# gMLP stage of a two-layer trunk: the split of v's normalised tiles written behind u's first block pair

## The chip, the cores and the metric

The kernel runs on one core of a Trainium2 chip. The metric is the device time of one execution in microseconds (us); for the kernel before it is the median of three runs. The profile is of one further execution.

## The reference, cut to what matters

The trunk is two layers over 512 tokens of width 1024. Layer 0 has a stick-breaking attention mixer, layer 1 a token-mixing MLP (gMLP); a SwiGLU network follows each mixer, and each of these four parts stands between two RMS norms with shift, scale and gate from a conditioning vector. The change is in layer 1's mixer:

```
def token_mixing_mixer(h, w_in, ln_g, w_s, b_s, w_out):
    B, S, D = h.shape
    uv = jax.nn.gelu(h @ w_in)
    u, v = jnp.split(uv, 2, axis=-1)
    v = layer_norm(v, ln_g)
    n = S // TM_CHUNK
    v = v.reshape(B, n, TM_CHUNK, TM_GROUPS, TM_GROUP_DIM)
    ...
    sv = jnp.einsum('gts,bnsgc->bntgc', ws, v) + b_s.T[None, None, :, :, None]
    y = u * sv.reshape(B, S, D)
    return y @ w_out
```

## The kernel before, in words

All matrix products keep float32 accuracy by splitting. A float32 tile is split into a high part (a copy into a reduced float32 type, on ScalarE) and a low part (the tile less its high part, on VectorE); a product is then three matmuls, high by high, low by high and high by low (`mm3`, line 122). Every matmul is recorded by `mm` at line 111, every ScalarE activation or copy at line 89, and nearly every VectorE operation at line 73, so that in the profile the names of the tiles tell them apart.

The gMLP stage is `gmlp`, line 1655. It runs in this order:

- v, in four tiles `vt` of 128 tokens by 1024 channels. The first 512 channels come from plain products, the last 512 by a scheme of seven block products (lines 1690 to 1707) that accumulate in three PSUM banks (`r`); each value passes through gelu.
- the statistics of the layer norm, per token (lines 1718 to 1725, `bns`, `mv`, `sd`, `r`), and the normalisation of the four `vt` tiles in place on VectorE (line 1735).
- the split of each normalised tile: high part `vnh` on ScalarE (line 1740), low part `vnl` on VectorE (`vn_low`, line 1728). The low parts of tiles 0 and 1 stand in the text right there; those of tiles 2 and 3 stand behind the first and the second block pair of u (line 1795), with an order dependency on the last VectorE operation written before them.
- u, in eight column blocks m. Block 0 was made earlier. Blocks 1 and 2, and then 3 and 4, are made as two block pairs by `u_pair` (line 1584), each with seven block products in three PSUM banks (R1, R2, R3, all named `r` in the profile). ScalarE copies three partial sums out of the banks into `e` (s1, s5, u1 of lines 1610, 1615 and 1617), VectorE combines them with what the banks hold next (lines 1612, 1619, 1621), and the bank is then accumulated on or written again by the next product. So some products can only start when such a copy or combination has read the bank. Blocks 5 to 7 are plain products (`u_unit`, line 1565).
- the mixing: `mix` (line 1746) multiplies each group of `vnh` and `vnl` with the mixing matrix `ws` into PSUM (`sv`); the first call comes behind u's block 5 (line 1800). The gating `u * sv` and the output projection (`part`, `out_proj`) follow.

Each engine executes its own instructions in a fixed order. In this stage that order is not written by hand: it is set, when the program is built, by a scheduler that starts from the text's order and each instruction's dependencies. The order of TensorE, VectorE and ScalarE is written by hand only in other stages (chains switched on at lines 1395 and 1190). Tiles called `slot` come from one pool of 28 buffers (line 45) that are handed out in the order of the text, so moving a `slot` call also shifts which buffer a tile gets.

Weights arrive by DMA on SyncE's queue (`load`, line 127), and their splits (`wh`, `wl`) are made ahead of their use on the same ScalarE and VectorE that work on v and u. Partial sums of the next layer's modulation rows (`bg.step`, tiles `acch`, `accl`, `adaps`, `A`, `B`) are mixed in.

Of the kernel before, what the change touches and what calls it, by code (L numbers as in the profile page):

```python
# [9 lines left out]
F32R = mybir.dt.float32r  # L10
AF = mybir.ActivationFunctionType
# [4 lines left out]
NT = T // P  # L16
# [19 lines left out]
def trunk(ctx: ExitStack, tc: tile.TileContext, A: dict, out: bass.AP):  # L36
# [17 lines left out]
    def nm(s):  # L54
        uid[0] += 1
        return f"{s}_{uid[0]}"

    def slot(dt, name, a=2, b=512):
        return s4.tile([P, a, b], dt, tag="s4", name=nm(name))

    def bank(name, tag="b"):
        return psum.tile([P, 512], F32, tag=tag, bufs=6 if tag == "b" else 2, name=nm(name))
# [32 lines left out]
    act = Scalar()  # L95
# [7 lines left out]
    def order(b, before):  # L103
        tc.add_manual_dep(
            b.ins, before.ins.name,
            mybir.DependencyInfo(mybir.DependencyClass.NoSync, mybir.DependencyReason.DATA),
            reason="order",
        )
# [13 lines left out]
    def mm3(o, lh, ll, rh, rl, start, stop):  # L122
        mm(o, lh, rh, start, False)
        mm(o, lh, rl, False, False)
        mm(o, ll, rh, False, stop)
# [221 lines left out]
    def wget(src, look=3):  # L347

        n = taken[0]
        taken[0] += 1  # L350
        while len(got) < min(n + 1 + look, len(stream)):
            wemit()
        assert stream[n][3] == src, (stream[n][3], src)
        return got[n]
# [199 lines left out]
    def hB(hT, k, lo, n):  # L554

        h, l = hT[lo // 256, k // 4]
        lo %= 256
        return h[:, k % 4, lo : lo + n], l[:, k % 4, lo : lo + n]
# [428 lines left out]
    with tc.tile_pool(name="att", bufs=1) as att, tc.tile_pool(name="att2", bufs=2) as att2:  # L987
# [62 lines left out]
        for js in (B31, B2, B0):  # L1050
            at, n = {}, 0
# [147 lines left out]
        for k in range(KD):  # L1199
# [9 lines left out]
            if k > 3:  # L1209
                tt = TURNS[k - 4]  # L1210
# [373 lines left out]
    def u_pair(hT, S, n):  # L1584

        W = wget(("blocks", ("u", n)), 0)
        R1, R2, R3 = [bank(r)[:, :256] for r in ("r1", "r2", "r3")]
        lo, hi = slice(0, 256), slice(256, T)
        a, b = 1 + 2 * n, 2 + 2 * n
        for m in (a, b):  # L1590
            if m // 2 == len(u4):
                u4.append(slot(F32, "u"))
        ua, ub = [u4[m // 2][:, m % 2, :] for m in (a, b)]
        e = fwork["pool"].tile([P, 768], F32, tag="e", name=nm("e"))[:]
        s1, u1, s5 = [e[:, i * 256 : (i + 1) * 256] for i in range(3)]

        def product(o, x, w, start, stop):
            for k in range(4):
                if x in "1234":
                    h, l = [t[:, k, :] for t in S[x]]  # L1600
                else:
                    h, l = hB(hT, k + 4 * (x[2] == "2"), 256 * (x[1] == "2"), 256)
                wh, wl = W[w](k)
                mm3(o, wh, wl, h, l, start and k == 0, stop and k == 3)

        def gelu(o, src):
            last_act[0] = act.activation(o, src, AF.Gelu_apprx_tanh)

        product(R1, "A11", "B11", True, False)
        act.activation(s1, R1, AF.Copy)  # L1610
        product(R2, "A12", "B21", True, True)
        dve.tensor_tensor(ua[:, lo], R2, s1, ALU.add)
        gelu(ua[:, lo], ua[:, lo])
        product(R3, "1", "T1", True, False)
        act.activation(s5, R3, AF.Copy)
        product(R1, "2", "T2", False, False)
        act.activation(u1, R1, AF.Copy)
        product(R3, "4", "B22", False, True)
        dve.tensor_tensor(ub[:, lo], R3, u1, ALU.subtract)
        product(R1, "3", "T3", False, False)  # L1620
        dve.tensor_tensor(ub[:, hi], s5, R1, ALU.subtract)
        gelu(ub, ub)
        product(R1, "A22", "T4", False, True)
        gelu(ua[:, hi], R1)

    STEPS = 2
    vt, v0 = {}, {}
# [27 lines left out]
    def gmlp(bg, hT, nhT, nS, nxt):  # L1655
# [70 lines left out]
        vn = []  # L1726

        def vn_low(tt, after=None):
            h, l = [a[:, 0, :] for a in vn[tt]]
            b = dve.tensor_tensor(l, vt[tt][:, 0, :], h.bitcast(F32), ALU.subtract)  # L1730
            if after is not None:
                order(b, after)

        for tt in range(NT):
            dve.tensor_scalar(
                vt[tt][:, 0, :], vt[tt][:, 0, :], mv[:, tt, 0:1], r[:, tt : tt + 1],
                ALU.subtract, ALU.mult,
            )
            vn.append((slot(F32R, "vnh", 1, 1024), slot(F32R, "vnl", 1, 1024)))
            act.activation(vn[tt][0][:, 0, :], vt[tt][:, 0, :], AF.Copy)  # L1740
            if tt < 2:
                vn_low(tt)

        shifts = {}

# [46 lines left out]

        for n in range(UPAIRS):
            u_pair(hT, S2, n)
            vn_low(2 + n, dve.prev)
            bg.step(6)
        for m in range(1 + 2 * UPAIRS, KD):
# [24 lines left out]
        [lambda: v_first(hT2, (0, 1)), lambda: v_first(hT2, (2, 3)), lambda: u_first(hT2)], S2,  # L1822
    )
    gmlp(bg2, hT2, hT3, S3, f1.first())
    f1.last(Bg("G3", slots=1))

# [103 lines left out]
```

## Time and profile before

| | us |
|---|---|
| median of 3 runs | 1096.84 |
| lowest and highest of them | 1094.85 and 1097.35 |
| the profiled execution, its own time | 1098.4 |
| its span, from the first to the last instruction | 1096.6 |
| TensorE busy in it | 1084.6 |
| VectorE busy in it | 971.7 |
| ScalarE busy in it | 611.7 |
| u's first block pair starts on TensorE | 666.50 |
| first matmul that reads vnh | 693.32 |
| the four vnh copies start | 674.22 to 682.7 |

The profiled execution took 1.8 us more than its span; all times of single instructions below are from the span's start. PE is TensorE (its matmuls), PEld its weight loads, DVE VectorE, ACT ScalarE, POOL GpSimd, SP SyncE. A matmul row gives its start and how long it was under way; matmuls overlap, so what tells the rate is the distance from start to start, the pitch.

### The profile page before, as it was taken

Reading aid. Unit: us, or ns where it says so; the run is one execution under the profiler, and the core shown is the slowest. Engines: PE = TensorE matmul, PEld = TensorE weight load, DVE = VectorE, ACT = ScalarE, POOL = GpSimd, SP = SyncE. Lnnn points to the kernel's source line nnn. Section 1 sums busy time; section 2 is a strip of 40 time slices with the busy share of each in tenths; the row PEclk is TensorE's granted clock in tenths of the full one; section 3 lists DMA queues with packets and bytes.
Section 4 is the critical chain, followed back from the end, with each engine's and each line's share of the span. In section 5 each row is a group of like instructions: output and inputs, shape, how many; then the busy total and the mean of one; then the engine's idle time right before and its main releaser. Section 6 shows DMA issues by size and latency. Waiting matters only on the chain.

```text
span 1096.6 us, 18739 instructions
## 1 busy us (share of the span) xinstructions
PE 1084.6 (99%) x7474; PEld 981.7 (90%) x7474; DVE 971.7 (89%) x1297; ACT 611.7 (56%) x1015; POOL 28.1 (3%) x50
## 2 busy tenths in 40 slices
PE   9999999999999999999999999999999999999997
PEld 6877887888999999998888799988999999999996
DVE  5988999967889999989977999869979999899996
ACT  7545665656555555554253767536545555565662
POOL 0020100000000000000000000001000000000000
PEclk9999999999999999999999999999999999999999
DMA  8976424304424433369878424443324442233252
GB/s 329 383 234 198 146 94 152 117 20 153 149 103 164 145 134 139 119 215 341 299 250 299 146 78 139 149 144 146 128 104 154 146 159 99 103 111 97 77 193 77
DMA packets 51355, 176.38 MB, mean 161 GB/s; under 512 B 6074, under 2 KB 9146, under 8 KB 51268
## 3 DMA queue, kind: packets, MB, share of 16 engines
q1 hardware_dynamic: 48708, 166.81, 43.9%
q0 software_dynamic: 2560, 8.39, 2.0%
q8 instruction: 58, 0.95, 0.4%
q14 instruction: 29, 0.24, 0.1%
HBM read 164.69 MB, written 8.39 MB: 158 GB/s over the span
## 4 chain that ended last, share of the span: by engine, by line
PE 90%; DVE 4%; DMA 3%; ACT 2%; issue 1%; SPq 0%; DVEq 0%; ACTq 0%
PE r L111 36%; PE y L111 13%; PE pqk L111 7%; PE v L111 6%; PE gu L111 6%; PE X L111 4%; PE Y L111 3%; PE u L111 2%; PE av L111 2%; PE z L111 2%; PE tw L119 1%; PE Z L111 1%; PE W L111 1%; PE tp L119 1%; DMA raw<-in_wdown 1%; DMA x<-in_x 1%
## 5 line engine op out<-in xcount | busy, mean ns | idle before, releaser
L111 PE MATMUL r<-Sh,wh 128*128 128x256 f32 x640 | 177.1, 277 | 0.6 <-ACT e L89 0.6
L111 PE MATMUL r<-Sh,wl 128*128 128x256 f32 x640 | 176.9, 276 | 0.0
L111 PE MATMUL r<-Sl,wh 128*128 128x256 f32 x640 | 176.7, 276 | 0.0
L89 ACT ACTIVATE wh<-raw 128x1024 fp32r<-128x1024 f32 (+1 forms) x105 | 108.4, 1037 | 106.4 <-DMA raw<-in_wdown 33.3
L111 PE MATMUL y<-wh,as 128*128 128x512 f32 x480 | 150.4, 391 | 0.0
L111 PEld LDWEIGHTS r<-Sh,wh 128*128 128x128 f32 x640 | 120.2, 188 | 1.2 <-ACT e L89 1.0
L188 DVE TENSOR_TENSOR wl<-raw,wh 128x1024 fp32r<-128x1024 f32 x79 | 96.0, 1220 | 27.4 <-ACT wh L89 27.2
L111 PEld LDWEIGHTS r<-Sl,wh 128*128 128x128 f32 x640 | 120.2, 188 | 0.1
L111 PEld LDWEIGHTS r<-Sh,wl 128*128 128x128 f32 x640 | 120.1, 188 | 0.0
L73 DVE TENSOR_TENSOR wl<-f,wh 128x1024 fp32r<-128x1024 f32 x95 | 112.8, 1218 | 1.8 <-ACT wh L89 1.8
L89 ACT ACTIVATE wh<-f 128x1024 fp32r<-128x1024 f32 x95 | 100.2, 1055 | 16.9 <-DVE f L73 12.3
L111 PEld LDWEIGHTS y<-wh,as 128*128 128x128 f32 x480 | 90.0, 188 | 18.6
L89 ACT ACTIVATE e<-r 128x256 f32<-128x256 f32 x120 | 45.9, 384 | 102.0 <-PE r L111 100.9
L111 PE MATMUL y<-wl,as 128*128 128x512 f32 x240 | 93.7, 390 | 0.0
L111 PE MATMUL r<-hTh,wh 128*128 128x256 f32 x320 | 88.7, 277 | 0.0
L111 PE MATMUL r<-hTl,wh 128*128 128x256 f32 x320 | 88.4, 276 | 0.0
L111 PE MATMUL r<-hTh,wl 128*128 128x256 f32 x320 | 88.4, 276 | 0.0
L111 PE MATMUL r<-hTh,b 128*128 128x256 f32 x320 | 61.0, 276 | 0.0
L111 PEld LDWEIGHTS r<-hTh,wh 128*128 128x128 f32 x320 | 60.1, 188 | 0.9 <-DVE gu L73 0.7
L111 PEld LDWEIGHTS r<-hTl,wh 128*128 128x128 f32 x320 | 60.1, 188 | 0.0
L111 PEld LDWEIGHTS r<-hTh,wl 128*128 128x128 f32 x320 | 60.1, 188 | 0.0
L89 ACT ACTIVATE wh<-rawx 128x1024 fp32r<-128x1024 f32 x40 | 42.5, 1062 | 30.0 <-PE r L111 29.2
(295 smaller groups left out, 2928.8 us busy)
## 6 DMA issues: line engine op xcount, KB each, us to landing
rawada<-in_ada SPq DMA_DIRECT2D x80, 512.0 KB, 6.4
rawy<-in_wy SPq DMA_DIRECT2D x38, 512.0 KB, 4.3
rawx<-in_wx SPq DMA_DIRECT2D x38, 512.0 KB, 3.5
raw<-in_wdown SPq DMA_DIRECT2D x22, 512.0 KB, 5.3
raw<-in_wdn SPq DMA_DIRECT2D x22, 512.0 KB, 3.5
raw<-in_wqk SPq DMA_DIRECT2D x16, 512.0 KB, 4.6
ada<-in_ada0p SPq DMA_DIRECT2D x12, 512.0 KB, 7.9
raw<-in_wgu SPq DMA_DIRECT2D x12, 512.0 KB, 3.6
```

Source lines behind the costliest of these rows:

```text
L73: b = getattr(nc.vector, op)(*args, **kw)
L89: b = nc.scalar.activation(*args, **kw)
L111: b = nc.tensor.matmul(o, l, r, start=start, stop=stop, skip_group_check=True)
L119: last_tp[0] = nc.tensor.transpose(o, i, ident)
L188: last_low[0] = nc.vector.tensor_tensor(l[:], raw[:], h[:].bitcast(F32), ALU.subtract)
```

## The change

The allocation of the split tiles, the four high copies and the low parts of tiles 0 and 1 leave the loop that normalises v, and come back in the loop over u's block pairs, behind the first pair and ahead of the low part of tile 2. Nothing is added or removed.

```
                 vt[tt][:, 0, :], vt[tt][:, 0, :], mv[:, tt, 0:1], r[:, tt : tt + 1],
                 ALU.subtract, ALU.mult,
             )
-            vn.append((slot(F32R, "vnh", 1, 1024), slot(F32R, "vnl", 1, 1024)))
-            act.activation(vn[tt][0][:, 0, :], vt[tt][:, 0, :], AF.Copy)
-            if tt < 2:
-                vn_low(tt)
...
         for n in range(UPAIRS):
             u_pair(hT, S2, n)
+            for tt in range(NT if n == 0 else 0):
+                vn.append((slot(F32R, "vnh", 1, 1024), slot(F32R, "vnl", 1, 1024)))
+                act.activation(vn[tt][0][:, 0, :], vt[tt][:, 0, :], AF.Copy)
+                if tt < 2:
+                    vn_low(tt)
             vn_low(2 + n, dve.prev)
             bg.step(6)
```

The built order changes only in this stage, and each engine has as many instructions as before. Three places follow. The numbers at the names' ends differ between the two programs: u's first pair has the banks `r1_1129`, `r2_1130`, `r3_1131` before and `r1_1121`, `r2_1122`, `r3_1123` now, and its copies go to `e_1133` and `e_1125`; the second pair has `r1_1150`, `r2_1151`, `r3_1152` and `e_1154` in both; `u_1132` before is `u_1124` now.

First ScalarE, right behind the gelu of the first part of u's block 1 (`u_1055`). Before:

```order
L89 ACTIVATE vnh_1107_7053<-vt_1053_6667 128x1024
L89 ACTIVATE e_1133_7103<-r3_1131_7101 128x256
L89 ACTIVATE e_1133_7103<-r1_1129_7099 128x256
L89 ACTIVATE acch_1138_7208<-A_895_5921 128x512
L89 ACTIVATE wh_1148_7228<-f24_1147_7223 128x1024
L89 ACTIVATE e_1154_7237<-r1_1150_7233 128x256
L89 ACTIVATE wh_1162_7350<-raw_1161_7348 128x1024
L89 ACTIVATE b21_1340_8268<-rawy_1324_8235 128x512
L89 ACTIVATE wh_1165_7356<-raw_1164_7354 128x1024
L89 ACTIVATE e_1154_7237<-r3_1152_7235 128x256
L89 ACTIVATE vnh_1109_7058<-vt_1054_6669 128x1024
L89 ACTIVATE e_1154_7237<-r1_1150_7233 128x256
```

The same place on ScalarE now:

```order
L89 ACTIVATE e_1125_7089<-r3_1123_7087 128x256
L89 ACTIVATE e_1125_7089<-r1_1121_7085 128x256
L89 ACTIVATE acch_1138_7208<-A_895_5921 128x512
L89 ACTIVATE wh_1148_7228<-f24_1147_7223 128x1024
L89 ACTIVATE e_1154_7237<-r1_1150_7233 128x256
L89 ACTIVATE wh_1162_7350<-raw_1161_7348 128x1024
L89 ACTIVATE wh_1165_7356<-raw_1164_7354 128x1024
L89 ACTIVATE b21_1340_8268<-rawy_1324_8235 128x512
L89 ACTIVATE u_1124_7088<-u_1124_7088 128x512
L89 ACTIVATE u_1124_7088<-u_1124_7088 128x256
L89 ACTIVATE u_1055_6671<-r1_1121_7085 128x256
L89 ACTIVATE vnh_1126_7183<-vt_1053_6667 128x1024
```

The first `vnh` copy stood ahead of the copies s5 (out of `r3`) and u1 (out of `r1`) of the first pair; now it stands eleven places later, behind three gelus of u that stood behind all four `vnh` copies before. Next on ScalarE now come `e_1154` out of `r3_1152` (s5 of the second pair), the second `vnh`, `e_1154` out of `r1_1150` (its u1), and the third and fourth `vnh`.

Then TensorE, in the second pair's product into R2. Before:

```order
L111 MATMUL r2_1151_7234<-hTl_997_6409,b21_1143_7217 128x256
L111 MATMUL r2_1151_7234<-hTh_996_6408,b21_1144_7218 128x256
L111 MATMUL r3_1152_7235<-Sh_1060_6677,wh_1145_7220 128x256
L111 MATMUL r3_1131_7101<-Sh_1062_6679,wh_1119_7078 128x256
L111 MATMUL r3_1131_7101<-Sl_1063_6680,wh_1119_7078 128x256
```

Now:

```order
L111 MATMUL r2_1151_7234<-hTh_996_6408,b21_1143_7217 128x256
L111 MATMUL r2_1151_7234<-hTl_997_6409,b21_1143_7217 128x256
L111 MATMUL r3_1123_7087<-Sh_1062_6679,wh_1111_7064 128x256
L111 MATMUL r3_1123_7087<-Sl_1063_6680,wh_1111_7064 128x256
L111 MATMUL r3_1123_7087<-Sh_1062_6679,wl_1112_7065 128x256
```

The first pair's fifth product (into its R3, which needs the copy s5) came behind all 12 matmuls of the second pair's R2 product and one of its R3 product; now it comes behind 5 of the R2 product, eight matmuls earlier. The sixth product (into R1, 12 matmuls) follows it in both. Behind these two TensorE now has 7 matmuls into `r2_1151`, 5 into `r3_1152`, the first pair's last product (12 into `r1_1121`), 7 into `r3_1152`, three products of 12 of the second pair, the two of `adaps`, 13 of u's block 5 and the second pair's last product; before, the first pair's last product stood behind that `adaps`, and 8 of u's block 5 stood between it and the second pair's last.

Last VectorE, right behind the four normalisations of `vt`. Before:

```order
L73 TENSOR_TENSOR wl_1146_7221<-f13_1142_7215,wh_1145_7220 128x1024
L73 TENSOR_TENSOR accl_1139_7209<-A_895_5921,acch_1138_7208 128x512
L73 TENSOR_TENSOR wl_1149_7229<-f24_1147_7223,wh_1148_7228 128x1024
L188 TENSOR_TENSOR wl_1163_7351<-raw_1161_7348,wh_1162_7350 128x1024
L73 TENSOR_TENSOR vnl_1108_7054<-vt_1053_6667,vnh_1107_7053 128x1024
L73 TENSOR_TENSOR vnl_1110_7059<-vt_1054_6669,vnh_1109_7058 128x1024
L188 TENSOR_TENSOR wl_1166_7357<-raw_1164_7354,wh_1165_7356 128x1024
L73 TENSOR_TENSOR u_1132_7102<-r3_1131_7101,e_1133_7103 128x256
L73 TENSOR_TENSOR u_1132_7102<-e_1133_7103,r1_1129_7099 128x256
L73 TENSOR_TENSOR vnl_1112_7064<-vt_1071_6785,vnh_1111_7063 128x1024
L73 TENSOR_TENSOR u_1132_7102<-r2_1151_7234,e_1154_7237 128x256
L73 TENSOR_TENSOR u_1153_7236<-r3_1152_7235,e_1154_7237 128x256
```

The same place on VectorE now:

```order
L73 TENSOR_TENSOR u_1124_7088<-r3_1123_7087,e_1125_7089 128x256
L73 TENSOR_TENSOR accl_1139_7209<-A_895_5921,acch_1138_7208 128x512
L73 TENSOR_TENSOR wl_1146_7221<-f13_1142_7215,wh_1145_7220 128x1024
L73 TENSOR_TENSOR u_1124_7088<-e_1125_7089,r1_1121_7085 128x256
L73 TENSOR_TENSOR wl_1149_7229<-f24_1147_7223,wh_1148_7228 128x1024
L73 TENSOR_TENSOR u_1124_7088<-r2_1151_7234,e_1154_7237 128x256
L188 TENSOR_TENSOR wl_1163_7351<-raw_1161_7348,wh_1162_7350 128x1024
L188 TENSOR_TENSOR wl_1166_7357<-raw_1164_7354,wh_1165_7356 128x1024
L73 TENSOR_TENSOR vnl_1127_7184<-vt_1053_6667,vnh_1126_7183 128x1024
L73 TENSOR_TENSOR b21_1329_8244<-rawy_1322_8231,b21_1328_8243 128x512
L73 TENSOR_TENSOR vnl_1129_7188<-vt_1054_6669,vnh_1128_7187 128x1024
L73 TENSOR_TENSOR vnl_1131_7192<-vt_1071_6785,vnh_1130_7191 128x1024
```

The two combinations of the first pair's block 2 (`u` out of `r3` and of `r1`) move ahead of the low parts, the four `vnl` move behind both weight splits of line 188, and the low part `wl_1146` of the second pair's weights now stands behind one combination and `accl`. Next come the second pair's two combinations (`u_1153` out of `r3_1152` and of `r1_1150`), behind three `vnl`, and the fourth `vnl`. On SyncE and GpSimd nothing changes place.

## The prediction

> **What bounds the kernel now.** I read the page's busy times and chain first, then the waits of TensorE, then the stretch around the change engine by engine. In the page, the busy times and the chain's shares by engine:
>
> ```profile
> span 1096.6 us, 18739 instructions
> PE 1084.6 (99%) x7474; PEld 981.7 (90%) x7474; DVE 971.7 (89%) x1297; ACT 611.7 (56%) x1015; POOL 28.1 (3%) x50
> PE 90%; DVE 4%; DMA 3%; ACT 2%; issue 1%; SPq 0%; DVEq 0%; ACTq 0%
> ```
>
> TensorE is busy for 99% of the span and carries 90% of the chain. A change that leaves its matmuls alone can only gain where TensorE stands still, or lose by making it stand still. The waits of TensorE on the block products (total, times, longest) are one row:
>
> ```profile
> PE r L111 <- ACT e L89: 0.6, 2, 0.5
> ```
>
> Twice TensorE's `r` waited for ScalarE's copy `e`, 0.6 us in all. One of the two lies in the stage that changes. The stage by time (busy us of PE, PEld, DVE, ACT, POOL, then granted clock, DMA share and GB/s):
>
> ```profile
> 666.50:675.50 9.00, 8.91 (x77) 8.63 (x75) 8.80 (x19) 7.10 (x12) 0.00 (x0) 1.00 0.35 112
> 675.50:687.00 11.50, 11.41 (x94) 11.21 (x95) 11.50 (x16) 10.16 (x16) 0.00 (x0) 1.00 0.44 151
> ```
>
> TensorE lacks 0.09 us in each; VectorE is nearly full, ScalarE nine tenths. TensorE in this stage, at the rows that count (start, us, what; in brackets the idle time before):
>
> ```profile
> 672.42 0.28 PE L111 MATMUL r<-hTh,wh 128*128 128x256 f32 x1
> ...
> 675.14 0.28 PE L111 MATMUL r<-Sh,wh 128*128 128x256 f32 x1
> 675.59 0.39 PE L111 MATMUL r<-Sh,wh 128*128 128x256 f32 x1 [0.18 <-ACT e L89]
> 675.82 0.28 PE L111 MATMUL r<-Sl,wh 128*128 128x256 f32 x1
> ...
> 678.53 0.28 PE L111 MATMUL r<-Sl,wh 128*128 128x256 f32 x1
> ...
> 684.07 0.39 PE L111 MATMUL adaps<-acch,ones 128*128 128x512 f32 x1
> 684.30 0.40 PE L111 MATMUL adaps<-accl,ones 128*128 128x512 f32 x1
> 684.54 0.32 PE L111 MATMUL r<-hTh,wh 128*128 128x256 f32 x1
> ...
> 687.30 0.28 PE L111 MATMUL r<-hTh,wh 128*128 128x256 f32 x1
> ...
> 688.32 0.28 PE L111 MATMUL u<-hTh,wl 128*128 128x256 f32 x1
> ...
> 693.32 0.28 PE L111 MATMUL sv<-ws,vnh 128*128 128x256 f32 x1
> ```
>
> Matmuls overlap, so idle time understates a wait. From 672.42 to 675.14 are 24 matmuls: a pitch of 2.72/24 = 113.3 ns. After 675.14 the next was due at 675.25 and came at 675.59: the wait cost 0.34 us. Then the pitch is longer: from 675.82 to 678.53 are 23 matmuls, 117.8 ns each; from 678.53 to 684.07 are 47, 117.9 ns. From 687.30 to 688.32 are 9 at 113.3 ns again. A second, hidden wait shows in the weight loads:
>
> ```profile
> 684.47 0.19 PEld L111 LDWEIGHTS r<-hTh,wh 128*128 128x128 f32 x1 [0.20 <-DVE u L73]
> ```
>
> The first pair's last product into R1 waited for VectorE's `u`; the matmul came at 684.54, and due it was 0.23 us behind the `adaps` at 684.30 at the latest; I put the loss at 0.04 us at most. Nothing reads `vnh` before 693.32, so the moved work itself has slack.
>
> **What the change removes.** ScalarE before, and VectorE before:
>
> ```profile
> 673.90 0.42 ACT L89 ACTIVATE u<-u 128x256 f32<-128x256 f32 x1
> 674.22 1.05 ACT L89 ACTIVATE vnh<-vt 128x1024 fp32r<-128x1024 f32 x1
> 675.17 0.64 ACT L89 ACTIVATE e<-r 128x256 f32<-128x256 f32 x2
> 675.70 0.63 ACT L89 ACTIVATE acch<-A 128x512 fp32r<-128x512 f32 x1
> 676.22 1.06 ACT L89 ACTIVATE wh<-f 128x1024 fp32r<-128x1024 f32 x1
> ...
> 680.03 0.38 ACT L89 ACTIVATE e<-r 128x256 f32<-128x256 f32 x1
> ```
>
> ```profile
> 673.29 2.98 DVE L73 TENSOR_SCALAR vt<-vt,mv,r 128x1024 f32<-128x1024 f32 x4
> 676.18 1.22 DVE L73 TENSOR_TENSOR wl<-f,wh 128x1024 fp32r<-128x1024 f32 x1
> 677.32 0.68 DVE L73 TENSOR_TENSOR accl<-A,acch 128x512 fp32r<-128x512 f32 x1
> 677.92 1.22 DVE L73 TENSOR_TENSOR wl<-f,wh 128x1024 fp32r<-128x1024 f32 x1
> ...
> 683.67 0.41 DVE L73 TENSOR_TENSOR u<-r,e 128x256 f32<-128x256 f32 x1
> 684.00 0.41 DVE L73 TENSOR_TENSOR u<-e,r 128x256 f32<-128x256 f32 x1
> ```
>
> The first `vnh` copy delays s5 and u1 by one copy's pitch, 675.17 − 674.22 = 0.95 us. Now s5 starts at 674.22 and ends, at 0.38 us for one, at 674.60. Before, it ended at 675.17 + 0.38 = 675.55 and TensorE started 0.04 us later; so the wait would now end at 674.64. But TensorE also asks earlier: its product stands eight matmuls ahead, 17 behind 672.42, so it is due at 672.42 + 17 × 0.1133 = 674.35. The wait is 0.29 us instead of 0.34: the first term is **−0.05 us**. The 0.95 us are almost all given back, since the scheduler moved the asker with the copy.
>
> The second term is the hidden wait at 684.47. The first pair's last product now comes later relative to its combination (below), and I take its 0.04 us as gone: **−0.04 us**.
>
> **What it adds.** Every instruction is still there, so the only cost is in new waits; I lay the new order out with the durations above. Pitches: VectorE 1.14 us for 1024 wide (677.32 − 676.18), 0.60 for 512 (677.92 − 677.32), 0.33 for 256 (684.00 − 683.67); ScalarE 0.95, 0.52 (676.22 − 675.70) and about 0.3. TensorE takes 2.94 us for the 24 matmuls behind the wait (675.59 to 678.53), and 0.118 for each one after.
>
> TensorE: fifth and sixth product from 674.64 to 677.58; 7 into R2 of the second pair, then two into its R3: at 678.64 it asks for the low part `wl_1146`. VectorE starts the combination out of `r3` when the fifth product is done, 674.64 + 1.41 + 0.28 of the last matmul, about 676.36; then `accl` 676.69, `wl_1146` 677.29 to 678.51. Margin 0.13 us. Next the combination out of `r1`, 678.43 to 678.84; TensorE asks for that bank at 678.99. Margin 0.15 us. These two are the tight ones; queued behind them on TensorE is everything else, so a miss is paid in full, and the most that one can be missed by without another cause is the 0.60 of the `accl` put ahead of `wl_1146`.
>
> Then TensorE does the first pair's last product to 680.40, 7 matmuls to 681.23, the second pair's T2 product to 682.64, where it asks for s5 of the second pair. ScalarE is 0.95 us earlier than before up to `b21_1340` (678.38 to 678.9). Its next gelu waits for VectorE's 678.84, the one behind it for the combination out of `r2_1151` (VectorE: `wl_1149` from 678.76, `u` 679.90 to 680.31), the third for TensorE's 680.56 (last matmul 680.28 and 0.28). So `vnh` starts at about 680.98, and s5 runs from 681.93 to 682.31: margin 0.33 us. The second `vnh`, then u1 done at about 683.53, asked for at 684.05: margin 0.5. VectorE meanwhile: two weight splits, `vnl`, `b21_1329`, `vnl`, `vnl` (which waits for nothing), and the second pair's combinations at 686.53 and 686.86 to 687.27. TensorE asks for that at 684.05 + 1.41 + two `adaps` of 0.235 + 13 × 0.118 = 687.46. Margin 0.2. The fourth `vnl` ends at about 688.4, with 4.9 us to `sv`. All margins hold: **0**, with bounds of 0 and +0.6 by the row of `accl`.
>
> The last term is the long pitch. It lasted from 675.59 to about 687.2 here (the 113.3 ns above are from 687.30 on), some 95 matmuls × 4.5 ns = 0.43 us. It is not special to this place; the other wait of `r` for `e`, in layer 0's network, and the same products of layer 1's network, which have no wait:
>
> ```profile
> 312.19 0.39 PE L111 MATMUL r<-Sh,wh 128*128 128x256 f32 x1 [0.47 <-ACT e L89]
> ```
>
> ```profile
> 793.00:960.00 167.00, 167.00 (x1476) 167.00 (x1475) 152.29 (x200) 93.03 (x158) 0.00 (x0) 1.00 0.37 130
> ```
>
> Where nothing waits, 1476 matmuls take 167.00 us, 113.1 ns. So the long pitch seems to come with a wait; why it ends I cannot read from the trace. Since a wait stays, I take the term as **0**, bounded by −0.43 (it ends at once) and +0.3 (it lasts to 693.32, 52 matmuls more at 4.5 ns, and a little). [...]
>
> **The sum.** −0.05 − 0.04 + 0 + 0 = −0.1 us, ends −0.5 (−0.09 − 0.43) and +0.8 (−0.09 + 0.6 + 0.3). On the profiled execution: 1098.4 − 0.1 = 1098.3. That execution lies 1.6 us above the median of the runs, 1096.84, so for the median I say **1096.7 us**. A measurement of this kernel can tell about 0.2%, 2.2 us, from no change; the whole sum is far inside.
>
> **The rivals.**
> *The wait vanishes.* s5 is free to go ahead at 674.22; if ScalarE's gelu of `u` (673.90) came 0.3 us earlier, TensorE would not wait, and the pitch would stay short: −0.34 − 0.04 − 0.43 = −0.8 us, 1096.0. For it: the first `vnh` is gone from between. Against it: s5 also needs the gelu ahead of it done, whose start hangs on unchanged work. 0.15; this too is within 0.2%.
> *ScalarE gets stuck (slower).* Three gelus that wait for VectorE and TensorE now stand ahead of `vnh`, and `vnh` ahead of s5 of the second pair. If they come late, TensorE waits for s5 behind a whole copy. It decides from 0.33 us of lateness; at 2 us, which takes nearly two 1024-wide subtractions (1.14 each) of delay on VectorE, it costs 1.7 us, and with the longer pitch (0.3) and the same delay for the second pair's combinations (0.4 over the margin of 0.2) 2.4 us: 1099.2. For it: VectorE is 100% busy from 675.50 to 687.00. Against it: its order up to there is shorter than before by two `vnl`. 0.09, with half of that beyond 0.2%. [...]
> *The clock drops.* If short waits made the clock fall to half, the 24 products behind the wait would take 2.8 us more, 1099.5. Against it: the granted clock is 1.00 in the stretch with the wait. 0.01. [...]
> *The edit moves nothing that counts,* as the scheduler decides: the order shows that it did move `vnh`, but with the asker; that is my forecast, not another time.
>
> **How the numbers follow.** Forecast 0.69, wait gone 0.15, ScalarE stuck 0.09, clock 0.01; the remaining 0.06 for medians of few runs that stray or an effect not seen here, to both sides alike. Beyond 0.2%: slower 0.045 + 0.01 and almost nothing of the rest, 0.05; faster 0.03; within 0.2% 0.92. Range: three runs spread over 2.5 us, so a median may lie 1.2 to either side; with half of the wait-gone case below (0.5) and of the new waits above (0.6), 1095.0 to 1098.5.
>
> **What would show it.** In the profile after: the row of `r` waiting for `e` near 674.6 with about 0.2 us idle (right), or none (the first rival); the pitch behind it 118 or 113 ns; no wait on VectorE at `wl` or `u` near 678.6, 679.0 and 687.4; `sv` first at about 693.2. An idle of over 1 us near 682.6 before `r`, released by `e`, would be the second rival. I would be wrong if the stage from 666.50 to the first `sv` changed by over 1 us, or if time moved in a stage whose order has not changed.

## The result and the profile after

The kernel after takes 1098.23 us, median of 11 runs (1097.17 to 1100.41); the kernel before, beside it on the same chip, 1096.56 (11 runs). The ratio is 1.0019 with a 95% interval from 1.001 to 1.0027: about 2 us slower, within the 0.2% that I had called no change, but clear of zero, and not the 0.1 us gain of my sum. Ratios in this document leave out two executions that took far longer, one of 1194.9 us of the kernel before and one of 6211.78 us of the kernel g_ahead0 below.

One profiled execution of each hides this. The profiled one after took 1097.51 us, less than before's 1098.4. The waits of TensorE over the whole span say why. Before, then after (total, times, longest):

```profile
PE tp L119 <- DVE t L73: 1.5, 2, 1.2
```

```profile
PE adaps L111 <- DVE A L73: 1.1, 1, 1.1
PE tp L119 <- DVE t L73: 0.3, 1, 0.3
```

Before's execution lost 1.5 us at the transposes `tp` in front of the gMLP stage, in a part that both programs share; after's lost 0.3 there. New is the row above it: `adaps` waited 1.1 us for `A`. So I compare from the first `r` matmul of v on, in three stretches: to the first `sv`, to the last `sv`, to the end. First before, then after (stretch, its length, busy time and instructions of PE, PEld, DVE, ACT and POOL, granted clock, DMA share, GB/s):

```profile
646.28:693.32 47.04, 46.86 (x393) 46.29 (x391) 45.70 (x64) 35.26 (x55) 0.00 (x0) 1.00 0.39 125
693.32:720.25 26.93, 26.93 (x199) 25.35 (x198) 23.78 (x46) 11.77 (x16) 0.00 (x0) 1.00 0.30 96
720.25:1096.60 376.35, 369.21 (x2804) 351.14 (x2803) 337.45 (x469) 208.07 (x331) 3.09 (x5) 1.00 0.37 127
```

```profile
643.34:691.79 48.45, 47.31 (x392) 46.43 (x391) 45.85 (x64) 35.03 (x54) 0.00 (x0) 1.00 0.36 115
691.79:719.28 27.49, 27.49 (x200) 25.81 (x199) 23.80 (x45) 12.20 (x16) 0.00 (x0) 1.00 0.31 105
719.28:1095.70 376.42, 369.28 (x2804) 351.19 (x2803) 337.82 (x470) 208.09 (x331) 3.09 (x5) 1.00 0.37 126
```

The first stretch is 1.41 us longer, the second 0.56, the rest 0.07: 2.04 us, the size of the timed loss. Where the first one goes is in three engines' rows of the kernel after. SyncE's queue:

```profile
679.68 0.33 SPq L128 DMA_DIRECT2D raw<-in_wout  x1
682.55 0.33 SPq L128 DMA_DIRECT2D g<-in_pre_g  x1
```

VectorE:

```profile
681.31 2.35 DVE L73 TENSOR_TENSOR vnl<-vt,vnh 128x1024 fp32r<-128x1024 f32 x2
...
685.38 0.68 DVE L73 TENSOR_TENSOR accl<-B,acch 128x512 fp32r<-128x512 f32 x1
687.22 1.29 DVE L73 SCALAR_TENSOR_TENSOR A<-adaps,g 128x512 f32<-128x512 f32 x2 [1.16 <-DMA g<-in_pre_g]
688.42 1.22 DVE L188 TENSOR_TENSOR wl<-raw,wh 128x1024 fp32r<-128x1024 f32 x1
```

TensorE:

```profile
686.71 0.28 PE L111 MATMUL u<-hTh,wl 128*128 128x256 f32 x1
688.06 0.47 PE L111 MATMUL adaps<-acch,ones 128*128 128x512 f32 x1 [1.07 <-DVE A L73]
688.37 0.39 PE L111 MATMUL adaps<-accl,ones 128*128 128x512 f32 x1
```

Read from the bottom. `adaps` needs the PSUM bank that the first operation of `A` reads. `A` needs `g`, a row of the next layer's modulation, and stood for 1.16 us until its load landed. The row at 681.31 is the low parts of tiles 1 and 2. The load was issued at 682.55, as the first of them ended (681.31 + 1.22 = 682.53), and landed 4.6 us later. That is no accident: in the built program of the kernel after, `g` gets the `slot` buffer that `vt` of tile 1 leaves, and the low part is the last reader of that tile. Before, the order of the text gave `g` the buffer of a block sum (`Sh`), whose last reader is TensorE; it was issued at once behind the load ahead of it:

```profile
683.82 0.33 SPq L128 DMA_DIRECT2D raw<-in_wout  x1
684.20 0.42 SPq L128 DMA_DIRECT2D g<-in_pre_g  x1
```

Counted from the first `r`, that is 684.20 − 646.28 = 37.92 us before and 682.55 − 643.34 = 39.21 after, 1.29 us later; and `A` before, at 689.33, had no idle time ahead of it, since the load had landed at 688.62. The tile that had `g`'s buffer last in each kernel of this study, and its last reader, from the built programs:

```
before, late23, before_lateg, big_dose, before_s5    block sum Sh (read by TensorE)
after (all runs), g_halves, before_g0                vt of tile 1 (read by its low part on VectorE)
g_ahead0, g_ahead0_s5                                su, a partial sum of v, free early
```

### The profile page after: what moved, and what is told of

Same layout as the page of the kernel before. It is cut to its first block, busy times and chain, and to the rows that moved or that the text cites. A ratio compares the mean times of both kernels' runs of the same rounds, so it can differ in the third digit from the quotient of the medians.

```text
span 1095.7 us, 18737 instructions
## 1 busy us (share of the span) xinstructions
PE 1085.6 (99%) x7474; PEld 982.7 (90%) x7474; DVE 972.2 (89%) x1297; ACT 612.6 (56%) x1015; POOL 28.1 (3%) x50
```

## The experiments

Theory G: the loss is `g`'s late load, through `A` and `adaps`. Rivals: Q, a longer queue on SyncE or the transfer itself; S, the moved splits cost by themselves, whatever `g` does; R, what the longer ones of the timed executions lose stands elsewhere. For each profile the table gives the same stretches as above; the end is the span's. "Timed" is the ratio to the kernel before in runs on the same chip, less one, times 1097 us, with its interval.

| kernel | wait at adaps | r to sv | sv stretch | r to end, against 450.3 | timed |
|---|---|---|---|---|---|
| before | 0 | 47.04 | 26.93 | 0 | |
| after, four profiles | 1.1, 0.7, 0.4, 1.3 | 48.45, 48.20, 47.69, 48.69 | 27.49, 27.34, 27.43, 27.57 | +2.1, +1.7, +1.3, +2.4 | +2.1 [1.1, 3.0]; +3.3 [2.0, 4.7] |
| before_lateg | 0.7 | 47.84 | 26.93 | +0.9 | +0.9 [−0.1, 1.8] |
| g_halves | 0.6 | 47.98 | 27.71 | +1.8 | +2.6 [1.5, 3.7] |
| g_ahead0 | 0 | 46.93 | 27.01 | +0.1 | 0.0 [−1.0, 1.0] |
| late23 | 0 | 46.89 | 26.93 | 0.0 | −0.3 [−1.3, 0.7] |
| before_g0 | 0.6 | 47.83 | 27.01 | +1.0 | +1.1 [0.1, 2.1] |
| big_dose | 4.0 | 53.59 | 27.30 | +7.0 | +5.9 [4.2, 7.7] |
| before_s5 | 0 | 47.15 | 26.93 | +0.2 | −0.2 [−1.2, 0.9] |
| g_ahead0_s5 | 0 | 47.03 | 27.70 | +0.9 | +0.9 [0.0, 1.9] |

For every kernel the part of the profile from the first `r` on lies inside the timed interval, but for two profiles of after (+1.7 and +1.3), which lie below the second of its intervals. The total of one profiled execution doesn't serve, since the start of that stage scatters from 642.9 to 646.3 us.

**after_again**: the kernel after, unedited.

> The changed kernel once more. Theory G (the buffer of g): the row g is loaded into the buffer that vt of tile 1 leaves, so its load waits for that tile's low part; it lands too late for A, and the two adaps matmuls that need A's bank wait. It expects the same wait again: TensorE idle before adaps of 0.8 to 1.5 us, released by A on VectorE, and a ratio of 1.0010 to 1.0025. Rival Q (the queues): the moved copies and low parts themselves hold up ScalarE and VectorE; it expects the lost time at r, u or sv instead. Rival S (scatter): the loss is one of layout and DMA luck in stages that did not change; it expects the stage from u's first pair to sv to take the same time as before.

1099.35 us (6 runs), ratio 1.003 [1.0018, 1.0043]. The loss is there again, and so is the wait, at 0.72 us. Both lie just outside what I expected by G.

**before_lateg**: the kernel before with `g`'s load held back to about where the change puts it.

```
+                if late_g[0] is not None:
+                    order(nc.vector.memset(g[0:1, 0:1], 0.0), late_g[0])
+                    late_g[0] = None
                 load(g, row[s : s + 1, :].to_broadcast([P, D]))
...
             vn_low(2 + n, dve.prev)
+            late_g[0] = dve.prev if n == 0 else None
             bg.step(6)
```

> The kernel before, with one tiny VectorE write into g's buffer put right behind the low part of tile 2, so that g's load can only start behind it (about 685.5 us instead of 684.2 in the profile of before); the split of v stays where it was. Theory G: g lands at about 690.2 (4.64 us as after), A is done at about 691.0, and adaps, due at about 690.3, waits 0.6 to 1.5 us with A as the releaser; ratio 1.0005 to 1.0018. Rivals Q and S: the split is where it was, so no wait at adaps and a ratio of 1.0000 within 0.0006.

1097.23 us, ratio 1.0008 [0.9999, 1.0016]. The rows of `g`'s load, of `A` and of `adaps`:

```profile
683.06 0.33 SPq L129 DMA_DIRECT2D g<-in_pre_g  x1
```

```profile
687.72 1.29 DVE L74 SCALAR_TENSOR_TENSOR A<-adaps,g 128x512 f32<-128x512 f32 x2 [0.83 <-DMA g<-in_pre_g]
```

```profile
688.56 0.48 PE L112 MATMUL adaps<-acch,ones 128*128 128x512 f32 x1 [0.67 <-DVE A L74]
```

The late load alone makes the wait and lengthens the stretch to `sv` by 0.8 us; the `sv` stretch stays at 26.93. The timed difference of this kernel is not clear of zero; the wait and the stretch of its profile carry the reading. So G is real, and is not the whole loss.

**g_ahead0**: the kernel after with `g`'s load written ahead of the block pairs.

```
+        bg.row("A", 3, 1)
         for n in range(UPAIRS):
             u_pair(hT, S2, n)
```

> The changed kernel, with g's row asked for ahead of u's block pairs, so that it gets a buffer that has long been free and its load is issued at about 663 us; the split of v stays behind the first pair. The scheduler orders some matmuls of the two pairs differently. Theory G: no wait at adaps, ratio 0.9993 to 1.0006 against the kernel before. Rival Q: the moved split is still where the change put it, so the loss stays, 1.0010 to 1.0027. Rival S: anything from 0.999 to 1.002.

1097.14 us, ratio 1.0000 [0.9991, 1.0009]. The load leaves 20 us earlier and lands 5.6 us after its issue, and `A` no longer stands:

```profile
663.49 0.33 SPq L128 DMA_DIRECT2D g<-in_pre_g  x1
```

```profile
687.32 0.70 DVE L73 SCALAR_TENSOR_TENSOR A<-adaps,g 128x512 f32<-128x512 f32 x1
```

The splits are still moved, and the loss is gone: against S in its plain form. The transfer takes longer than in the kernel after (4.6 us) and costs nothing: against Q.

**g_halves**: the kernel after with `g` loaded in two transfers of 256 KB.

```
-                load(g, row[s : s + 1, :].to_broadcast([P, D]))
+                if (name, s) == ("A", 3):
+                    for c in (slice(0, 512), slice(512, D)):
+                        load(g[:, c], row[s : s + 1, c].to_broadcast([P, 512]))
+                else:
+                    load(g, row[s : s + 1, :].to_broadcast([P, D]))
```

> The changed kernel, with g loaded by two transfers of 256 KB (columns 0 to 511, then the rest) into the same late buffer; A's first half needs only the first. The scheduler puts the first adaps matmul 5 matmuls (0.57 us) earlier. Theory G: the first half lands 2.5 to 4.6 us behind the issue, so A's first half ends between 0.6 us earlier and the same time as in the changed kernel; the wait at adaps is 0.0 to 1.7 us, and the end of A sets it in any case; ratio 1.0000 to 1.0022. Rival Q: no change against the changed kernel, 1.0010 to 1.0027, with the wait not at adaps.

1099.21 us, ratio 1.0024 [1.0014, 1.0034]. The first half landed 3.65 us after its issue instead of 4.6, but the wait, 0.6 us, lies inside the 0.4 to 1.3 us of the unedited kernel, whose first matmul of `adaps` stands five matmuls later. It repaired nothing.

**after_p2** and **after_p3**: two more executions of the kernel after, with their traces.

> The changed kernel again, for one more execution with its trace: the timed runs of it lie between 1096.7 and 1100.9 us, and both profiled ones at the low end (1097.51 and 1096.71 us), with a wait of A for g's load behind which adaps lost 1.1 and 0.7 us. Theory G (the load of g, issued after the low part of tile 1, lands too late for A, and PE's adaps waits for A): the wait at adaps is there again, 0.5 us or more, and if this execution is slow (1099 us or more), the row for adaps is longer by about as much, 2 to 3 us, because g's landing takes longer than the 4.43 to 4.64 us seen so far. Rival R (the loss lies in another place and the wait at adaps is only a part of it): a slow execution shows the wait at adaps at 0.7 to 1.1 us as before, and 1 to 2 us more of idle PE elsewhere.

> The changed kernel once more, for the same question as the run ahead of it: by theory G the wait at adaps is 0.5 us or more and follows the landing of g, which varies from execution to execution; by rival R it stays at 0.7 to 1.1 us, and what a slow execution has lost stands elsewhere.

1097.15 and 1097.87 us; both are below the 1099 us from which the expectation sets G against R, so what the longer executions lose was not seen. But the wait did differ, with the landing of `g`. In after_p2, then in after_p3:

```profile
687.04 1.29 DVE L73 SCALAR_TENSOR_TENSOR A<-adaps,g 128x512 f32<-128x512 f32 x2 [0.50 <-DMA g<-in_pre_g]
```

```profile
687.46 1.29 DVE L73 SCALAR_TENSOR_TENSOR A<-adaps,g 128x512 f32<-128x512 f32 x2 [1.38 <-DMA g<-in_pre_g]
```

From 0.50 to 1.38 us of idle time the stretch to `sv` grows from 47.69 to 48.69 us, about one for one. This also showed what G leaves over: after_p2 waits only 0.4 us and is 1.3 us longer.

**late23**: the kernel before with half of the change; only the splits of tiles 2 and 3 are moved.

```
+        def vn_high(tt):
+            vn.append((slot(F32R, "vnh", 1, 1024), slot(F32R, "vnl", 1, 1024)))
+            act.activation(vn[tt][0][:, 0, :], vt[tt][:, 0, :], AF.Copy)
...
-            vn.append((slot(F32R, "vnh", 1, 1024), slot(F32R, "vnl", 1, 1024)))
-            act.activation(vn[tt][0][:, 0, :], vt[tt][:, 0, :], AF.Copy)
             if tt < 2:
+                vn_high(tt)
                 vn_low(tt)
...
             u_pair(hT, S2, n)
+            for tt in (2, 3) if n == 0 else ():
+                vn_high(tt)
             vn_low(2 + n, dve.prev)
```

> Half of the change: only the splits of tiles 2 and 3 are moved behind the first block pair of u; those of tiles 0 and 1 stay where they were. g's load then takes the buffer that the last low part of the weight split leaves, as in the kernel before, and waits for nothing that was moved. Theory G: no wait of A for g and none of adaps for A, time within 0.1% of the kernel before (1096.0 to 1098.1 us). Rival S (the loss comes from moving the splits of tiles 2 and 3 into the stretch ahead of sv): some 1 us or more slower than before, about 1098 us or above.

1096.74 us, ratio 0.9997 [0.9988, 1.0006], and no wait of TensorE in the stage. `g` is back in the block sum's buffer; G's forecast holds.

**before_g0**: the kernel before with the same early row as g_ahead0.

> The kernel before with one edit: the row for g's load stands ahead of the block pairs of u, so that the load is issued some microseconds earlier than its 684.2 us. Theory G: the kernel before had its adaps on time, so nothing is won at adaps; within 0.1% of the kernel before (1096.0 to 1098.1 us), and no wait of adaps for A. Rival R (g's load, wherever it stands, costs by what it collides with among the weight loads): a different time, 1 us or more to either side.

1098.2 us, ratio 1.001 [1.0001, 1.0019]: a miss of mine. The scheduler puts `A` and `adaps` earlier as well, and `g` now gets the buffer that `vt` of tile 1 leaves, so that its load again waits for that tile's low part. `A` stood for 0.74 us until it landed, and `adaps` waited behind `A`:

```profile
684.63 0.69 DVE L73 SCALAR_TENSOR_TENSOR A<-adaps,g 128x512 f32<-128x512 f32 x1 [0.74 <-DMA g<-in_pre_g]
```

```profile
685.46 0.47 PE L111 MATMUL adaps<-acch,ones 128*128 128x512 f32 x1 [0.60 <-ACT u L89]
```

The view names a gelu of ScalarE as the releaser (what ended the wait), since that is what ended last. But in the built program `adaps` waits for ScalarE only by the split that makes `acch`, which ended at 683.2, and for VectorE by the first operation of `A`; it starts 0.14 us behind the end of `A` (685.32), as in the kernel after (687.91 and 688.06). So the loss is G's chain once more, in a kernel that moves no split.

**big_dose**: before_lateg with the load later by two more writes of `g`'s tile on GpSimd, `adaps` held in its place.

```
+        if pin[1] is not None:
+            order(b, pin[1])
+            pin[1] = None
+        if pin[0] and not start and stop:
+            pin[:] = False, b
...
+                if late_g[0]:
+                    order(nc.vector.memset(g[0:1, 0:1], 0.0), late_g[0])
+                    late_g[0] = False
+                    for _ in range(2):
+                        nc.gpsimd.memset(g, 0.0)
                 load(g, row[s : s + 1, :].to_broadcast([P, D]))
...
+                    pin[0] = name == "B" and b == 0 and late_g[0] is False
```

> The kernel before with g's load delayed far more: as in the run with the late g, a one-element write on VectorE into g's tile stands behind the low part of tile 2, and two writes of the whole tile on GpSimd (0.96 us each by the rows of this program) follow it ahead of the load; the matmul that follows the third pair of adaps in the text is held behind that pair, so that the planner cannot push the pair back: it stands 26 matmuls of 113 ns, 2.9 us, earlier. It computes the same. Theory G (PE stands at adaps until g has landed and A is done, and every us of this wait is lost to the end): the late g's wait of 0.7 us grows by 2.0 and by 2.9 us to about 5.6 us, and the time to about 1102 to 1103.5 us. Rival S (the wait is made up for behind adaps, and the loss of the changed kernel comes from the order of the splits): a wait at adaps of several us in the trace, and a time of 1097 to 1099 us.

1102.63 us (4 runs), ratio 1.0054 [1.0038, 1.007], inside my figure, but not for my reasons alone. The wait was 4.0 us and not 5.6: `g` landed 3.65 us after its issue instead of 4.57 in before_lateg, and `adaps` was due 2.2 us earlier than there, not 2.9. The stretch is 6.5 us longer. TensorE, and the granted clock (the last number but two) behind the wait:

```profile
689.82 0.57 PE L113 MATMUL adaps<-acch,ones 128*128 128x512 f32 x1 [4.01 <-DVE A L75]
```

```profile
689.80:693.60 3.80, 3.79 (x17) 3.61 (x18) 2.85 (x4) 2.34 (x4) 0.00 (x0) 0.55 0.43 163
693.60:697.50 3.90, 3.90 (x35) 3.90 (x35) 1.36 (x2) 0.78 (x1) 0.00 (x0) 1.00 0.60 154
```

Behind the stop the clock was 0.55 for 3.8 us: some 14 matmuls 0.1 us late each, 1.4 us more. A further 0.5 us went to a wait of `r` for `u`. This speaks against S as it was put: none of the wait was made up for.

**before_s5** and **g_ahead0_s5**: the gelu of the first part of u written behind the copy s5, in the kernel before and in g_ahead0.

```
-        gelu(ua[:, lo], ua[:, lo])
         product(R3, "1", "T1", True, False)
         act.activation(s5, R3, AF.Copy)
+        gelu(ua[:, lo], ua[:, lo])
```

> The kernel before with the activation of the first half of u's block written behind the copy of s5, so that ScalarE reads s5's bank first and PE's next product into it does not wait. The splits stay where they were. The wait at that place, 0.34 and 0.11 us, goes, and with it perhaps the longer pitch of 117.8 instead of 113.3 ns behind it, 0.4 us in all: 1096.0 to 1096.6 us by the rival of my prediction in which this wait vanishes (-0.8 us); about 1096.9 us if the pitch stays long for other reasons or the wait moves to the next bank. Nothing of theory G is touched: no wait of adaps for A.

> The changed kernel with g's load ahead of the block pairs and s5's copy ahead of the activation: both waits that the traces show in this stage should be gone. Theory G: no wait of adaps for A, so it is not slower than the kernel before; with the s5 wait gone as well 0.3 to 0.8 us faster, 1096.1 to 1096.7 us. Rival S (moving the splits costs by itself): still some 1 us slower than the same edit in the kernel before.

1096.76 us, ratio 0.9998 [0.9989, 1.0008], and 1097.91, ratio 1.0008 [1.0, 1.0017]. In the first the wait did not vanish. Two smaller ones stand in its place, 0.08 and 0.06 us over the pitch:

```profile
671.06 0.28 PE L111 MATMUL r<-hTh,wl 128*128 128x256 f32 x1
671.25 0.38 PE L111 MATMUL r<-Sh,wh 128*128 128x256 f32 x1
...
674.03 0.28 PE L111 MATMUL r<-hTh,b 128*128 128x256 f32 x1
674.20 0.38 PE L111 MATMUL r<-Sh,wh 128*128 128x256 f32 x1
```

What that won was lost again at the hidden wait of the prediction, which grew. The first pair's last product waits for VectorE's `u`:

```profile
682.74 0.19 PEld L111 LDWEIGHTS r<-hTh,wh 128*128 128x128 f32 x1 [0.40 <-DVE u L73]
```

Its matmul came 0.13 us late and the one behind it 0.11, and the pitch, back at 113 ns from 675 to 682 us, was 118 from there on to the first `sv`. The stretch is no shorter than before (47.15).

The second missed: `adaps` waits for nothing, yet 0.9 us slower, all of it but 0.1 in the `sv` stretch. So that stretch has a loss of its own. VectorE there, in the kernel before and in g_ahead0_s5:

```profile
703.04 1.21 DVE L188 TENSOR_TENSOR wl<-raw,wh 128x1024 fp32r<-128x1024 f32 x1
704.18 0.48 DVE L73 SCALAR_TENSOR_TENSOR svt<-sv,cols,svt 128x256 f32<-128x256 f32 x1
704.69 0.69 DVE L73 TENSOR_TENSOR u<-u,svt 128x512 f32<-128x512 f32 x1
```

```profile
701.64 1.22 DVE L188 TENSOR_TENSOR wl<-raw,wh 128x1024 fp32r<-128x1024 f32 x1 [0.79 <-ACT wh L89]
702.78 0.48 DVE L73 SCALAR_TENSOR_TENSOR svt<-sv,cols,svt 128x256 f32<-128x256 f32 x1
703.29 0.69 DVE L73 TENSOR_TENSOR u<-u,svt 128x512 f32<-128x512 f32 x1
```

This gating product `u` starts 704.69 − 693.32 = 11.37 us after the first `sv` before, and 703.29 − 690.48 = 12.81 us in g_ahead0_s5, because a weight split ahead of it waits 0.79 us for ScalarE's half, and that half 1.25 us for its load. The four profiles of after have 12.60, 12.47, 12.56 and 12.71, g_halves 12.85; their `sv` stretches are 27.49, 27.34, 27.43, 27.57 and 27.71, each 14.86 to 14.89 us more than this number, as in g_ahead0_s5 (27.70). In g_ahead0 and before_g0, at 12.12 and 12.15, the stretch is 27.01; below 12, as in late23 (11.95), it is 26.93, but for big_dose (10.77), whose pitch is 118 ns and whose stretch is 27.30. So in these runs, beyond about 12 us, VectorE sets the `sv` stretch, by freeing the banks of `sv`: in the kernel after one `sv` matmul came 0.21 us behind the one ahead of it (711.28 and 711.49); the same pair before stands 0.06 us apart (712.46 and 712.52). The rows of the kernel after read the same:

```profile
702.74 1.23 DVE L188 TENSOR_TENSOR wl<-raw,wh 128x1024 fp32r<-128x1024 f32 x1 [0.58 <-ACT wh L89]
...
704.39 0.69 DVE L73 TENSOR_TENSOR u<-u,svt 128x512 f32<-128x512 f32 x1
```

The weights are late since each split frees the buffer of a later load, and the first of these splits stands later: it ended at 689.42 before and a load of `raw` was issued at 689.44; in the kernel after at 689.64 and 689.67. In the kernel before, that split is the first row here:

```profile
688.20 1.22 DVE L188 TENSOR_TENSOR wl<-raw,wh 128x1024 fp32r<-128x1024 f32 x1
689.33 1.28 DVE L73 SCALAR_TENSOR_TENSOR A<-adaps,g 128x512 f32<-128x512 f32 x2
```

It stood ahead of `A`, 5.1 us before the first `sv`. In the kernel after, the scheduler has both operations of `A` ahead of it (VectorE's rows above), and the split, at 688.42, stands 3.4 us before the first `sv`. The moved low parts are not what is new: all four `vnl` stand ahead of this split in both kernels, and before_g0, which moves no `vnl` but has `A` ahead of the split as well, reads 12.15 like g_ahead0. So S holds in another form: not the splits' own time costs, but the order that the scheduler makes behind them.

In three of the four profiles of after a second cause lies on top of this one. There the matmuls of `u` in the `sv` stretch run at 118 ns, which alone makes TensorE 0.4 us late by the third group of `sv`, as in big_dose. In after_p2, at the short pitch, VectorE alone makes 0.5 us. This second part of the loss is read from the traces of all these kernels; none of them changed it alone.

## Why the prediction was wrong, point by point

- *"On SyncE and GpSimd nothing changes place"* and *"the moved work itself has slack"*: here it failed. The order on SyncE is indeed unchanged, and nothing reads `vnh` before the first `sv`. But I asked only who reads what the moved instructions write. The low part also ends the reading of `vt`, and so frees a buffer. The front of this document says that moving a `slot` call shifts buffers; I never followed who got which, and my schedule has no `A` in it. The term for new waits, 0 with bounds of 0 and +0.6, measured +0.4 to +1.3 us of wait at `adaps` alone, shown by before_lateg, before_g0, g_ahead0 and late23.
- The same step also passed over the weight splits that follow on VectorE, which now stand behind `A`. The `sv` stretch grew by 0.4 to 0.6 us, in part by this. The sign of being wrong that I had named came too: the stage up to the first `sv` changed by over 1 us.
- *The s5 wait.* Forecast 0.34 to 0.29 us. `r` came 0.34 us after the one ahead instead of 0.45, 0.23 us late instead of 0.34: right in kind. In the kernel after:

```profile
671.29 0.28 PE L111 MATMUL r<-hTl,b 128*128 128x256 f32 x1
671.63 0.39 PE L111 MATMUL r<-Sh,wh 128*128 128x256 f32 x1
```

- *The second pair's s5, margin 0.33 us.* Missed: `vnh` began at 678.38, where my schedule, moved by the 2.94 us that this execution started the stage earlier, gave 678.04. ScalarE read s5 at 679.35, and TensorE came 0.16 us late. With the matmul behind it, which follows 0.22 instead of 0.11 us later, this cost 0.27 us: my slower rival, "ScalarE gets stuck", at a ninth of its price.

```profile
679.50 0.28 PE L111 MATMUL r<-Sh,wl 128*128 128x256 f32 x1
679.77 0.39 PE L111 MATMUL r<-Sh,wh 128*128 128x256 f32 x1
679.99 0.28 PE L111 MATMUL r<-Sl,wh 128*128 128x256 f32 x1
```

This too is a buffer that changed hands. In the built program of the kernel after, the first `vnh` gets the `slot` buffer of a block sum (`Sl`), and that sum's last reader is the last but one matmul of the product that s5 copies; before, it got the one of `su`, free early. That matmul ended at 678.30, and the copy started behind it. ScalarE read s5 behind the copy, at 679.35, 0.97 us after the copy's start, though the product's last matmul ended at 678.42:

```profile
678.02 0.28 PE L111 MATMUL r<-Sl,wh 128*128 128x256 f32 x1
678.14 0.28 PE L111 MATMUL r<-Sh,wl 128*128 128x256 f32 x1
```

```profile
678.38 1.06 ACT L89 ACTIVATE vnh<-vt 128x1024 fp32r<-128x1024 f32 x1 [0.28 <-ACT u L89]
679.35 0.36 ACT L89 ACTIVATE e<-r 128x256 f32<-128x256 f32 x1
```

- *The rival "the wait vanishes", −0.8 us.* before_s5 tried its cause directly: the wait only split in two, another one grew, and no gain can be told. So its case, a pair without a wait, was not reached, and its price stays untested.
- *The margins on VectorE.* The first, 0.13 us for `wl` near 678.6, was missed by a hair. The low part ended at 674.37 + 1.22 = 675.59, TensorE's matmul came at 675.64, 0.02 us late, and the next one 0.23 us behind it instead of 0.11. At the other two, near 679.0 and 687.4, no wait showed.

```profile
675.51 0.28 PE L111 MATMUL r<-Sl,wh 128*128 128x256 f32 x1
675.64 0.39 PE L111 MATMUL r<-Sh,wl 128*128 128x256 f32 x1
675.87 0.28 PE L111 MATMUL r<-Sh,wh 128*128 128x256 f32 x1
```

- *The long pitch.* In the kernel after it ended at 675.9, earlier than before, and came back behind the wait at `adaps`, 118 ns up to the third group of `sv`, in three of four profiles, and not in after_p2, whose wait was 0.4 us. Within my bounds in the first stretch; why it comes and ends stays open.

The first stretch adds up, from the due times: `adaps`, due at 686.71 + 0.11, came 1.24 us late, and its first matmul took 0.31 instead of 0.23 us (0.08), the second s5 0.27, `wl` 0.11, the first s5 −0.11, the hidden wait −0.04, and the long pitch, which makes up 0.31 us of the stretch instead of 0.43, −0.12: 1.43, measured 1.41. So 1.3 of the 1.4 us is the one wait that I had not looked for, and the other misses nearly cancel. That timed runs of after lie somewhat above its four profiled ones (1096.71 to 1097.87 us) is not explained; the scatter of the stage's start, which both programs share, is as large.

No kernel here beat the one before by more than can be told.

## What to carry to other kernels

When an instruction is moved, ask not only who reads what it writes, but what its reading sets free, and which load or matmul takes that buffer or bank next; where a pool hands out buffers in the order of the text, list them for both programs. Where a view names a releaser that has nothing to do with the waiting instruction, the built program tells what that instruction really waits for. A queue whose order is the same can still start later, as `g`'s load did here by 1.29 us. And compare two profiles stage by stage from a common instruction on, since one execution's total carries waits of parts that the change doesn't touch (here 1.5 and 0.3 us at `tp`).

## What the runs showed of the hardware

Behind TensorE's stop of 4.01 us in big_dose the granted clock was 0.55 over 3.8 us, and the matmuls of `u` from 690.60 to 693.38 came 2.78/13 = 214 ns apart. Behind the stops of 1.07 us in the kernel after (688.00 to 691.70) and of 1.30 us in after_p3 it was 1.00. In after_p3:

```profile
688.30:692.00 3.70, 3.70 (x29) 3.61 (x30) 3.70 (x5) 1.12 (x2) 0.00 (x0) 1.00 0.29 61
```

So the longest wait of this change left the clock at 1.00: my rival "the clock drops" did not come about, and no run shows its 2.8 us for short waits. Between 1.3 and 4.0 us nothing was measured. And the load of `g`, 512 KB, landed 4.42 us after its issue before, 4.64 in the kernel after, 3.65 in big_dose and 5.8 in g_ahead0_s5; before, `A` started 0.71 us behind the landing (689.33 and 688.62), so that a start 1.29 us later was enough for `A` to stand.
